# Head pairs in turns, three-pass scores and another tile order in the first output projection of a diffusion backbone

## The chip, the cores and the metric

The kernel runs on one core of a Trainium2 chip. The metric is the device time of one execution in microseconds, as the median of three runs. On the core, TensorE multiplies (its weight loads are shown as an engine of their own, PEld), VectorE (DVE), ScalarE (ACT) and GpSimd (POOL) compute, and SyncE (SP) and ScalarE issue the DMA transfers here. TensorE's results land in eight banks of PSUM, from which the other engines read.

## The reference

Two layers over 256 latent tokens of width 1024 and 256 context tokens. Each layer is a mixer and an expert retrieval (PEER), each behind a modulated RMS norm:

```python
f, p, q, k, v, gates = split_proj(h @ w_in[l])            # and the same for the context tokens
ya = latent_attention(q, k_all, v_all) @ attn_proj[l]     # 8 heads of 64, 2 key/value heads, keys of latents and context
yf, yp = fourier_branch(f, fourier_w[l]), pool_branch(p, ...)
x = x + m_lat[2] * merge(yf, yp, ya, gates, w_out[l])     # (gates[0]*yf + gates[1]*yp + gates[2]*ya) @ w_out
...
yac = attend(qc, kc, vc)                                  # context tokens see context keys; not in the last layer
x = x + m_lat[5] * peer(h2, peer_wq[l], peer_keys[l], peer_u[l], peer_v[l])

def attend(q, k, v):
    s = einsum('bqhgd,bkhd->bhgqk', q, k) * (HEAD_DIM ** -0.5)
    return einsum('bhgqk,bkhd->bqhgd', softmax(s), v)
```

Everything is float32. The last layer needs no context output, so it has two token tiles of 128 where layer 0 has four (tiles 0 and 1 latent, 2 and 3 context).

## The kernel before

**Arithmetic.** The large products are made of two halves: a matrix is split into a high part, rounded to `fp32r`, and the rest (`split_to`, L286 to L289: ScalarE copies the high part, VectorE or GpSimd subtracts). `mm3` (L281 to L284) then adds three single-speed matmuls, high by high, high by low and low by high. Products of plain float32 tiles run as two steps each on TensorE. In the attention, scores (L667) and value products (L700) are such float32 products.

**Weights.** `Stream` loads the weights in a fixed order through three `raw` tiles of 1 MB. `take` issues the loads of the tile taken and of the two behind it; `split` hands out a tile's two halves, and `presplit` splits the next item ahead of its use. SyncE issues these loads in the order in which the program names them, and a load waits until its `raw` tile was read.

**Attention.** `mixer` transposes keys into `kT` and queries into `qT` (64 rows for each head, two heads on 128 partitions) and goes over `items`: head pair `hc`, token tile `b`, head `e` of the pair. Layer 0 has 32 items, 16 of them wide (latent tiles, four key tiles) and 16 narrow (context tiles, two key tiles); layer 1 has 16 wide ones. A written pipeline spreads an item over four turns of the loop: `stage_scores` (product, maximum on VectorE, exponential with sum on ScalarE), `stage_norm` (scaling on VectorE), `stage_T` (transposes on TensorE, copy on ScalarE) and `stage_pv` (value products). Head `e` writes columns `64*e` to `64*e+63` of the array into the bank `ya`. Between these stages `fill` puts 32 steps of six gate matmuls each: eight ahead of the key transposes, 24 spread over the loop. Their results wait in the four gate buffers of `store`.

**Output projection, layer 0.** `wout(n, b)` makes columns `256*n` to `256*n+255` of token tile `b` (24 matmuls, then a product and a sum on VectorE, L1254 and L1255). `wout_end(b)` stores the tile (L1258) and computes its norm (`Norm.row`: square on ScalarE, L434, a chain of small operations on VectorE, L297 to L305, and the scaling L442). `Norm.trans` transposes a norm's tiles (L451); `Norm.cols` modulates them (L472, L474) and splits them into `hTh` and `hTl`, for the latents (0) or the context (1). `keys` transposes the retrieval keys (L1229). Behind this, `peer` begins: three conditioning products of the next layer (`ada_item`, L333), which use the first bank of a new PSUM layout, then the query products of the first retrieval head, over the latents' columns first (`h == 0`), then the context's `cols` and their columns.

**Order.** The order of the work on each engine is the order in which the program names it; there is no scheduler.

Of the kernel before, what the change touches and what calls it, by code (L numbers as in the profile page):

```python
# [60 lines left out]
def kernel(ctx_: ExitStack, tc: tile.TileContext, I, C, out):  # L61
    nc = tc.nc
# [32 lines left out]
    def b8(shape, dt=F32, name="b8"):  # L95
        return b8_p.tile(shape, dt, tag="b8", name=name)

    def b4(shape, dt=F32, name="b4"):
        return b4_p.tile(shape, dt, tag="b4", name=name)
# [4 lines left out]
    def psum(shape=(128, 512), dt=F32, name="ps"):  # L104
        return banks["ps"].tile(list(shape), dt, tag="ps", name=name)
# [374 lines left out]
    def mixer(l, nrm, last):  # L480
# [78 lines left out]
                nc.vector.tensor_tensor(out=v, in0=v, in1=rope[:, b, 0:1, :].to_broadcast([128, nh, HD]), op=OP.mult)  # L559
                nc.vector.tensor_tensor(out=src, in0=src, in1=t, op=OP.add)  # L560

        kT = b4([128, 512], name="kT")
        qT = b8([128, 4, nt], name="qT")
        for b in range(4):
            rot(b, KV[:, b, :128], 8, 2)
            if b < nq:
# [73 lines left out]
                yield from gate_sums(u, lambda c, ps, n=n: nc.scalar.activation(store[:, n, c, :], ps, AF.Copy), True)  # L640

        filler = fill()
        for _ in range(8):
            next(filler)
        ps = psum()
        for b in range(4):
            nc.tensor.transpose(ps[:, b * 128:(b + 1) * 128], KV[:, b, :128], ident)
        nc.scalar.activation(kT, ps, AF.Copy)
        for j in range(4):
            ps = psum()  # L650
            for b in range(nq):
                nc.tensor.transpose(ps[:, b * 128:(b + 1) * 128], P[:, b, 512 + j * 128:640 + j * 128], ident)
            nc.scalar.activation(qT[:, j, :], ps[:, :nt], AF.Copy)

        items = [(hc, b, e) for hc in range(4) for b in range(nq) for e in range(2)]
        st = {}
# [2 lines left out]
        def stage_scores(n):  # L659
            hc, b, e = items[n]  # L660
            h = 2 * hc + e
            v, j = divmod(h, 4)
            kb = (0, 4) if b < 2 else (2, 4)
            nk = (kb[1] - kb[0]) * 128
            ps = psum()
            s = slice(64 * v, 64 * v + 64)
            nc.tensor.matmul(ps[:, :nk], lhsT=qT[s, j, b * 128:(b + 1) * 128], rhs=kT[s, kb[0] * 128:kb[1] * 128],  # L667
                             start=True, stop=True)
            mx = small([128, 3], name="mx", bufs=6)
            nc.vector.tensor_reduce(out=mx[:, 0:1], in_=ps[:, :nk], op=OP.max, axis=AX)  # L670
            nc.vector.tensor_scalar(mx[:, 0:1], mx[:, 0:1], -0.125, None, op0=OP.mult)
            pm = ring[:, n % 4, :]
            nc.scalar.activation(pm[:, :nk], ps[:, :nk], AF.Exp, bias=mx[:, 0:1], scale=0.125, accum_out=mx[:, 1:2])
            st[n] = (pm, mx, kb, nk)
# [15 lines left out]
        ya = {}  # L690

        def stage_pv(n):
            hc, b, e = items[n]
            v = (2 * hc + e) // 4
            pT, kb = st.pop(n)
            if b == 0 and e == 0:
                ya[hc] = psum(name="ya")
            for q in range(kb[0], kb[1]):
                o = (q - kb[0]) * 128
                nc.tensor.matmul(ya[hc][64 * e:64 * e + 64, b * 128:(b + 1) * 128],  # L700
                                 lhsT=KV[:, q, 128 + 64 * v:192 + 64 * v], rhs=pT[:, o:o + 128],
                                 start=q == kb[0], stop=q == kb[1] - 1)
            if b == nq - 1 and e == 1:
                split_to(yh[:, 4 + hc, :], yl[:, 4 + hc, :], ya.pop(hc)[:, :nt])

        N = len(items)
# [1 line left out]
        if l:  # L708
            ffn_rows(l)
        for n in range(N + 3):  # L710
            if 0 <= n - 1 < N:
                stage_norm(n - 1)
            if n < N:
                stage_scores(n)
            while filled < min(24 * (n + 1) // N, 24):
                next(filler, None)
                filled += 1
            if 0 <= n - 2 < N:
                stage_T(n - 2)
            if n >= 3:  # L720
                stage_pv(n - 3)
        for _ in filler:
            pass
# [494 lines left out]
    for l in range(DEPTH):  # L1218
# [38 lines left out]
        def wout_end(b):  # L1257
            nc.sync.dma_start(out=xm[b], in_=X[:, b, :])  # L1258
            nrm.row(b // 2, b % 2)
# [5 lines left out]
                wout(n, b)  # L1265
        if nb == 4:
            wo[2] = S.split(("wout", l, 2))
            for b in range(nb):
                wout(2, b)
            wo[3] = S.split(("wout", l, 3))  # L1270
            kr = S.take(("keys", l)).rearrange("p (a d) -> p a d", d=128)
            for b in range(2):
                wout(3, b)
            wout_end(0)
            wout(3, 2)
            wout_end(1)
            S.presplit(True)
            wout(3, 3)
            kT = keys()
            for q in range(4):  # L1280
                nrm.trans(0, q)
            for b in (2, 3):
                wout_end(b)
            for q in range(4):
                nrm.cols(0, q)
        else:
            wo[2] = S.split(("wout", l, 2))
            wo[3] = S.split(("wout", l, 3))
            kr = S.take(("keys", l)).rearrange("p (a d) -> p a d", d=128)
            wout(2, 0)  # L1290
            wout(3, 0)
            wout_end(0)
            S.presplit(True)
            wout(2, 1)
            wout(3, 1)
            wout_end(1)
            kT = keys()
            for q in range(4):
                nrm.cols(0, q)
# [70 lines left out]
```

## Time and profile before

| | |
|---|---|
| median of 3 runs | 2943.49 us (2942.41 to 2950.72) |
| profiled execution | 2943.76 us; its span from first to last instruction 2942.0 us |
| busy share of the span | TensorE 94%, its loads 82%, VectorE 73%, ScalarE 47%, GpSimd 44% |
| mean granted TensorE clock | 0.97 of full speed |
| chain that ended last, by engine | TensorE 23%, VectorE 8%, DMA 5%, ScalarE 2% |

The page gives busy time by engine and the chain of work that ended last; the trace gives, for any stretch, the instructions in order of time, the idle time ahead of each and what ended it. Matmuls are pipelined: a row's length holds the way through the array, so what a matmul costs in a row of matmuls is read from start to start. The two attention loops are about 103 and 61 us of the span.

### The profile page before, as it was taken

What the parts mean: (1) busy time and instruction counts of PE and PEld (TensorE: products, weight loads), DVE (VectorE), ACT (ScalarE), POOL (GpSimd) and SP (SyncE); (2) the same over time, 40 slices, a digit from 0 to 9 for tenths busy, and PEclk for the clock granted to TensorE, in tenths of its full rate; (3) what the DMA queues carried; (4) which work ended last, traced back from release to release, by engine and by line L of the source; (5) the groups of instructions that cost most, each with busy time, mean ns of one, the idle gap of its engine ahead of it and who ended that gap; (6) DMA issues with size and microseconds to landing.
All of it is one profiled execution on the core that took longest, in us unless ns stands there. A gap on an engine that the chain in (4) does not pass through costs nothing. (4 is left out here: it accounts for less than half of the span.)

```text
span 2942.0 us, 42776 instructions
## 1 busy us (share of the span) xinstructions
PE 2753.4 (94%) x16484; PEld 2403.8 (82%) x16484; DVE 2158.2 (73%) x3388; ACT 1375.9 (47%) x2243; POOL 1282.2 (44%) x698
## 2 busy tenths in 40 slices
PE   6999998799899999999999997998989989899999
PEld 4767786689888889988888886788989989888887
DVE  3444344899999985589999996555988778566666
ACT  3343223134489983333333334545446766544443
POOL 0110003237777778676666662102677655500000
PEclk8999998899999999999999999999999999899999
DMA  6215756558999999999999994337788898967775
GB/s 232 87 44 177 253 186 187 157 120 210 258 286 296 291 297 286 268 361 377 379 376 380 369 362 173 119 123 189 157 194 191 223 223 208 249 250 299 280 296 198
DMA packets 365580, 706.99 MB, mean 240 GB/s; under 512 B 25424, under 2 KB 265456, under 8 KB 351296
## 3 DMA queue, kind: packets, MB, share of 16 engines
q1 hardware_dynamic: 271104, 491.38, 56.0%
q0 software_dynamic: 36864, 134.23, 12.5%
q10 hardware_dynamic: 57408, 78.65, 7.9%
q8 instruction: 129, 2.11, 0.3%
q14 instruction: 75, 0.61, 0.1%
HBM read 619.18 MB, written 85.00 MB: 239 GB/s over the span
## 5 line engine op out<-in xcount | busy, mean ns | idle before, releaser
L1180 PE MATMUL acc<-hl,A 128*128 128x512 f32 x3840 | 871.2, 389 | 0.0
L1180 PEld LDWEIGHTS acc<-hl,A 128*128 128x128 f32 x3840 | 720.6, 188 | 150.1 <-ACT A L287 0.5
L1025 POOL TENSOR_TENSOR hl<-UT,hl 128x1024 fp32r<-128x1024 f32 x256 | 629.1, 2483 | 301.0 <-ACT hl L1018 298.9
L289 POOL TENSOR_TENSOR hl<-raw,hl 128x1024 fp32r<-128x1024 f32 x112 | 277.9, 2492 | 695.4 <-ACT hl L287 575.6
L287 ACT ACTIVATE hl<-raw 128x1024 fp32r<-128x1024 f32 x388 | 387.9, 1048 | 251.2 <-PE acc L1180 77.6
L289 DVE TENSOR_TENSOR hl<-raw,hl 128x1024 fp32r<-128x1024 f32 x276 | 349.8, 1299 | 133.5 <-ACT hl L287 133.2
L1011 DVE STREAM_TRANSPOSE UT<-raw 128x2048 f32<-128x2048 f32 x128 | 294.3, 2301 | 173.1 <-DMA raw<-in_peer_u_dram 115.0
L282 PE MATMUL ps<-hTh,hl 128*128 128x384 f32 (+2 forms) x1168 | 407.9, 349 | 4.2 <-ACT hl L1018 4.2
L284 PE MATMUL ps<-hTh,hl 128*128 128x384 f32 (+2 forms) x1168 | 402.0, 344 | 6.1 <-POOL hl L1025 6.1
L283 PE MATMUL ps<-hTl,hl 128*128 128x384 f32 (+2 forms) x1168 | 401.7, 344 | 3.5 <-POOL hTl L289 3.5
L284 PE MATMUL ps<-hT,hl 128*128 128x256 f32 x1152 | 333.7, 290 | 9.8 <-POOL hl L1025 9.8
L282 PE MATMUL ps<-hT,hl 128*128 128x256 f32 x1152 | 337.7, 293 | 1.6 <-ACT hl L1018 1.6
L283 PE MATMUL ps<-hT,hl 128*128 128x256 f32 x1152 | 333.3, 289 | 1.1 <-POOL hT L289 1.1
L1018 ACT ACTIVATE hl<-UT 128x1024 fp32r<-128x1024 f32 x256 | 256.6, 1051 | 140.1 <-DVE UT L1011 116.8
L287 ACT ACTIVATE A<-af 128x768 fp32r<-128x768 f32 (+1 forms) x128 | 94.4, 738 | 333.3 <-PE acc L1180 178.2
L282 PEld LDWEIGHTS ps<-hTh,hl 128*128 128x128 f32 x1168 | 224.8, 192 | 20.9 <-issue 4.9
L284 PEld LDWEIGHTS ps<-hT,hl 128*128 128x128 f32 x1152 | 228.4, 198 | 11.6 <-POOL hl L1025 11.6
L284 PEld LDWEIGHTS ps<-hTh,hl 128*128 128x128 f32 x1168 | 224.6, 192 | 12.1 <-POOL hl L1025 7.4
L283 PEld LDWEIGHTS ps<-hTl,hl 128*128 128x128 f32 x1168 | 225.1, 193 | 8.0 <-POOL hTl L289 3.7
L282 PEld LDWEIGHTS ps<-hT,hl 128*128 128x128 f32 x1152 | 229.6, 199 | 2.0 <-ACT hl L1018 2.0
L289 DVE TENSOR_TENSOR A<-af,A 128x768 fp32r<-128x768 f32 (+1 forms) x128 | 142.9, 1117 | 119.5 <-ACT A L287 119.5
L283 PEld LDWEIGHTS ps<-hT,hl 128*128 128x128 f32 x1152 | 229.0, 199 | 1.6 <-POOL hT L289 1.6
(245 smaller groups left out, 4795.8 us busy)
## 6 DMA issues: line engine op xcount, KB each, us to landing
raw<-in_peer_u_dram SPq DMA_DIRECT2D x512, 256.0 KB
raw<-in_peer_v_dram SPq DMA_DIRECT2D x128, 1024.0 KB
raw<-in_ada_w_dram SPq DMA_DIRECT2D x48, 1024.0 KB
G<-stg ACTq DMA_DIRECT2D x20, 2048.0 KB
raw<-in_w_in_dram SPq DMA_DIRECT2D x34, 1024.0 KB
Gq<-G SPq DMA_DIRECT2D x16, 1536.0 KB
H<-Hg ACTq DMA_DIRECT2D x56, 384.0 KB
Hq<-H SPq DMA_DIRECT2D x14, 1536.0 KB
```

The source lines that it names most:

```text
L282: nc.tensor.matmul(ps, lhsT=lh, rhs=rh, start=first, stop=False)
L283: nc.tensor.matmul(ps, lhsT=lh, rhs=rl, start=False, stop=False)
L284: nc.tensor.matmul(ps, lhsT=ll, rhs=rh, start=False, stop=last)
L287: nc.scalar.activation(hi, src, AF.Copy)
L289: eng.tensor_tensor(out=lo, in0=src, in1=hi.bitcast(F32), op=OP.subtract)
L1011: nc.vector.transpose(t, r)
L1018: nc.scalar.activation(t[:, 0, a], v[:, a], AF.Copy)
L1025: nc.gpsimd.tensor_tensor(out=t[:, 1, a], in0=v[:, a], in1=t[:, 0, a].bitcast(F32), op=OP.subtract)
L1180: nc.tensor.matmul(acc[b][n], lhsT=a4[:, lhs, a, t], rhs=rhs[:, o:o + 512], start=f, stop=e)
```

## The change

Four edits, all in the program's order or in the form of its products:

- `kT` and `qT` become pairs of high and low halves (`split_to` out of PSUM, with VectorE's subtraction), and a score is three `mm3` matmuls in place of one float32 product.
- `stage_pv` runs every second turn and does both heads of a pair, key tile by key tile, head 0 and head 1 in turns.
- In the loop `stage_scores(n)` stands ahead of `stage_norm(n - 1)`; of the eight filler steps ahead of the transposes four stay there, and one stands behind each of the four groups of query transposes.
- In layer 0's output projection the last two column blocks go tile by tile for the latents, then the context tiles; the keys' transposes, the latents' transposes and `cols` are placed between the context's products.

The gate buffers (`fills`, `store`) are the same before and after.

```diff
-        for _ in range(8):
+        for _ in range(4):
             next(filler)
         ps = psum()
         for b in range(4):
             nc.tensor.transpose(ps[:, b * 128:(b + 1) * 128], KV[:, b, :128], ident)
-        nc.scalar.activation(kT, ps, AF.Copy)
+        kT = [b4([128, 512], F32R, name="kT") for _ in range(2)]
+        qT = [b8([128, 4, nt], F32R, name="qT") for _ in range(2)]
+        split_to(kT[0], kT[1], ps)
         for j in range(4):
             ps = psum()
             for b in range(nq):
                 nc.tensor.transpose(ps[:, b * 128:(b + 1) * 128], P[:, b, 512 + j * 128:640 + j * 128], ident)
-            nc.scalar.activation(qT[:, j, :], ps[:, :nt], AF.Copy)
+            split_to(qT[0][:, j, :], qT[1][:, j, :], ps[:, :nt])
+            next(filler)
...
-            nc.tensor.matmul(ps[:, :nk], lhsT=qT[s, j, b * 128:(b + 1) * 128], rhs=kT[s, kb[0] * 128:kb[1] * 128],
-                             start=True, stop=True)
+            qh, ql = (t[s, j, b * 128:(b + 1) * 128] for t in qT)
+            kh, kl = (t[s, kb[0] * 128:kb[1] * 128] for t in kT)
+            mm3(ps[:, :nk], qh, ql, kh, kl, True, True)
...
         def stage_pv(n):
-            hc, b, e = items[n]
-            v = (2 * hc + e) // 4
-            pT, kb = st.pop(n)
-            if b == 0 and e == 0:
+
+            hc, b, _ = items[n]
+            v = 2 * hc // 4
+            if b == 0:
                 ya[hc] = psum(name="ya")
+            two = [st.pop(n - 1), st.pop(n)]
+            kb = two[0][1]
             for q in range(kb[0], kb[1]):
                 o = (q - kb[0]) * 128
-                nc.tensor.matmul(ya[hc][64 * e:64 * e + 64, b * 128:(b + 1) * 128],
-                                 lhsT=KV[:, q, 128 + 64 * v:192 + 64 * v], rhs=pT[:, o:o + 128],
-                                 start=q == kb[0], stop=q == kb[1] - 1)
-            if b == nq - 1 and e == 1:
+                for e, (pT, _) in enumerate(two):
+                    nc.tensor.matmul(ya[hc][64 * e:64 * e + 64, b * 128:(b + 1) * 128],
+                                     lhsT=KV[:, q, 128 + 64 * v:192 + 64 * v], rhs=pT[:, o:o + 128],
+                                     start=q == kb[0], stop=q == kb[1] - 1)
+            if b == nq - 1:
...
         for n in range(N + 3):
+            if n < N:
+                stage_scores(n)
             if 0 <= n - 1 < N:
                 stage_norm(n - 1)
-            if n < N:
-                stage_scores(n)
...
-            if n >= 3:
+            if n >= 3 and n % 2 == 0:
                 stage_pv(n - 3)
...
             wo[2] = S.split(("wout", l, 2))
-            for b in range(nb):
-                wout(2, b)
             wo[3] = S.split(("wout", l, 3))
             kr = S.take(("keys", l)).rearrange("p (a d) -> p a d", d=128)
             for b in range(2):
+                wout(2, b)
                 wout(3, b)
-            wout_end(0)
+                wout_end(b)
+            S.presplit(True)
+            wout(2, 2)
             wout(3, 2)
-            wout_end(1)
-            S.presplit(True)
-            wout(3, 3)
             kT = keys()
+            wout(2, 3)
             for q in range(4):
                 nrm.trans(0, q)
+            for q in range(4):
+                nrm.cols(0, q)
+            wout(3, 3)
             for b in (2, 3):
                 wout_end(b)
-            for q in range(4):
-                nrm.cols(0, q)
```

TensorE in layer 0's attention, before, where the loop passes from wide to narrow items (`ring` holds the exponentials and their transposes, `gate` is the filler; a row's x counts matmuls of the program; a value product and a score of before are two steps each on TensorE):

```order
L685 MATMUL ps<-ident,ring 128x128 x4
L700 MATMUL ya<-ring,KV 64x128 x4
L667 MATMUL ps<-kT,qT 128x256
L685 MATMUL ps<-ident,ring 128x128 x4
L700 MATMUL ya<-ring,KV 64x128 x4
L667 MATMUL ps<-kT,qT 128x256
L282 MATMUL gate<-hTh,hl 128x512
```

The same place in the changed kernel:

```order
L282 MATMUL ps<-kT,qT 128x256
L283 MATMUL ps<-kT,qT 128x256
L284 MATMUL ps<-kT,qT 128x256
L687 MATMUL ps<-ident,ring 128x128 x4
L705 MATMUL ya<-ring,KV 64x128 x8
L282 MATMUL ps<-kT,qT 128x256
L283 MATMUL ps<-kT,qT 128x256
L284 MATMUL ps<-kT,qT 128x256
L282 MATMUL gate<-hTh,hl 128x512
```

Two groups of four value products, each behind its own transposes, became one of eight, and a score became three matmuls.

VectorE at the end of layer 0's output projection, before (`tm` and `X` are the last product's two operations, `na` to `xn` tile 3's norm, `hTf` and `hTl` the latents' columns):

```order
L1254 TENSOR_TENSOR tm<-ps,mrow 128x256
L1255 TENSOR_TENSOR X<-X,tm 128x256
L297 TENSOR_SCALAR na<-ss 128x1
L300 RECIPROCAL nr<-nr 128x1
L302 TENSOR_TENSOR nt<-nr 128x1
L303 TENSOR_TENSOR nt<-nt,na 128x1
L304 TENSOR_SCALAR nt<-nt 128x1
L305 TENSOR_TENSOR nr<-nr,nt 128x1
L442 TENSOR_SCALAR xn<-X,nr 128x4x8x32
```

The same engine in the changed kernel, from the latents' columns on:

```order
L472 TENSOR_SCALAR hTf<-ps,sc_2907,col_2905 128x256 x2
L289 TENSOR_TENSOR hTl<-hTf,hTh 128x2x256
L472 TENSOR_SCALAR hTf<-ps,sc_2907,col_2905 128x256 x2
L289 TENSOR_TENSOR hTl<-hTf,hTh 128x2x256
L1259 TENSOR_TENSOR tm<-ps,mrow 128x256
L1260 TENSOR_TENSOR X<-X,tm 128x256
L297 TENSOR_SCALAR na<-ss 128x1
L300 RECIPROCAL nr<-nr 128x1
```

The latents' columns, which stood behind the norms of tiles 2 and 3, now stand ahead of the last product's two operations and of both norms.

## Rows read from the trace of the kernel before

**Rows 1.** Windows: both attention loops, the idle stretch, the conditioning products; busy us.

```profile
core 0: us, PE busy (x) PEld busy (x) DVE busy (x) ACT busy (x) POOL busy (x), PEclk, DMA share, GB/s
135.20:238.60 103.40, 102.40 (x497) 66.45 (x496) 44.50 (x131) 47.52 (x114) 15.26 (x8) 1.00 0.11 37
1873.40:1934.00 60.60, 60.48 (x368) 42.79 (x368) 27.85 (x67) 31.17 (x67) 16.09 (x7) 1.00 0.22 70
446.60:455.30 8.70, 0.03 (x3) 0.04 (x3) 6.29 (x19) 5.49 (x14) 2.88 (x3) 0.70 0.94 347
455.30:460.50 5.20, 5.20 (x24) 1.09 (x24) 1.14 (x1) 0.40 (x1) 1.48 (x2) 0.51 0.23 70
```

**Rows 2.** Timeline of TensorE, layer 0's loop: start us, length us, line, shape, count.

```profile
151.70 1.09 PE L700 MATMUL ya<-ring,KV 128*64 128x128 f32 x8
152.72 0.70 PE L667 MATMUL ps<-kT,qT 64*128 64x256 f32 x2
153.34 0.50 PE L282 MATMUL gate<-hTh,hl 128*128 128x512 f32 x1
153.68 0.39 PE L283 MATMUL gate<-hTl,hl 128*128 128x512 f32 x1
153.91 0.39 PE L284 MATMUL gate<-hTh,hl 128*128 128x512 f32 x1
...
158.59 0.65 PE L700 MATMUL ya<-ring,KV 128*64 128x128 f32 x4
159.17 1.12 PE L667 MATMUL ps<-kT,qT 64*128 64x512 f32 x2
```

**Rows 3.** Timeline of TensorE, layer 1's loop, its first score.

```profile
1873.44 1.12 PE L667 MATMUL ps<-kT,qT 64*128 64x512 f32 x2
1874.49 0.38 PE L282 MATMUL gate<-hTh,hl 128*128 128x256 f32 x1
1874.71 0.28 PE L283 MATMUL gate<-hTl,hl 128*128 128x256 f32 x1
1874.83 0.28 PE L284 MATMUL gate<-hTh,hl 128*128 128x256 f32 x1
```

**Rows 4.** Timeline of TensorE: Fourier products (full columns) and band products (two halves).

```profile
112.20 3.62 PE L592 MATMUL ps<-p,raw 128*128 128x256 f32 x16
115.75 3.73 PE L604 MATMUL ps<-raw,P 128*64 128x256 f32 x32
```

**Rows 5.** Timeline of TensorE behind layer 0's output projection; in brackets idle time before.

```profile
442.97 1.91 PE L1229 MATMUL ps<-ident,raw 128*128 128x128 f32 x16
...
455.29 5.29 PE L333 MATMUL adaps<-raw,cT 128*32 128x512 f32 x24 [8.67 <-DVE hTf L472]
460.50 0.39 PE L282 MATMUL ps<-hTh,hl 128*128 128x256 f32 x1
```

**Rows 6.** Timelines of ScalarE and VectorE: the latents' columns, first and later operations.

```profile
449.98 1.00 ACT L474 ACTIVATE hTf<-ps,col,sc 128x256 f32<-128x256 f32 x2
...
453.43 0.69 DVE L289 TENSOR_TENSOR hTl<-hTf,hTh 128x512 fp32r<-128x512 f32 x1 [0.70 <-ACT hTh L287]
...
455.73 1.14 DVE L289 TENSOR_TENSOR hTl<-hTf,hTh 128x512 fp32r<-128x512 f32 x1 [0.70 <-ACT hTh L287]
```

**Rows 7.** Timeline of SyncE's DMA issues: third conditioning tile, next query weights.

```profile
447.99 0.33 SPq L198 DMA_DIRECT2D raw<-in_ada_w_dram  x1
...
458.37 1.80 SPq L204 DMA_DIRECT2D raw<-in_peer_wq_dram  x4
```

**Rows 8.** Timelines of ScalarE, GpSimd and TensorE: what the context's columns wait for.

```profile
465.71 2.01 ACT L287 ACTIVATE hl<-raw 128x1024 fp32r<-128x1024 f32 x2 [10.01 <-DMA raw<-in_peer_wq_dram]
...
466.85 4.67 POOL L289 TENSOR_TENSOR hl<-raw,hl 128x1024 fp32r<-128x1024 f32 x2 [10.07 <-ACT hl L287]
...
473.24 0.58 PE L283 MATMUL ps<-hTl,hl 128*128 128x256 f32 x1 [3.52 <-POOL hTl L289]
```

**Rows 9.** Instructions on tile `mx`: the scaling of L679, ns min/median/max.

```profile
L679 DVE TENSOR_SCALAR ring<-ring,mx x48: 352/486/2186, 139.6 to 1929.2; 128x512 f32<-128x512 f32 x32, 128x256 f32<-128x256 f32 x16
```

More of the change, by code (lines that the diff above doesn't have):

```diff
@@ L560, in rot @@
                 nc.vector.tensor_tensor(out=src, in0=src, in1=t, op=OP.add)
-        kT = b4([128, 512], name="kT")
-        qT = b8([128, 4, nt], name="qT")
         for b in range(4):
```

## The prediction

> **What bounds the kernel now.** I read the stretches first, then the matmuls in order of time in each stretch that the change touches, then the queues around the one hole found there. [rows 1] give the two attention loops (layer 0 from the first score at 135.2 us to 238.6, layer 1 from 1873.4 to 1934.0): TensorE is busy 102.4 of 103.4 us and 60.5 of 60.6 at the full clock, while VectorE, ScalarE and GpSimd are each busy less than 53% of the time and the DMA engines 11 and 22%. So what these loops cost is what TensorE issues in them, and what is taken off TensorE there comes off the loop as long as VectorE and ScalarE keep up. Nothing is prefetched further meanwhile, since three raw tiles are all there are, so a shorter loop shifts what follows and takes nothing from it. The end of layer 0's output projection is another kind of place: [rows 5] show TensorE done with the projection at 442.97, then transposing, then idle for the 8.67 us ahead of 455.29 (so from 446.6) until VectorE has read the last transposed norm tile, then three conditioning products in 5.2 us, and the first query product at 460.50. In that hole and behind it the granted clock is 0.70 and 0.51 [rows 1]: the lower level (1.2 GHz, against 2.4) stands from inside the hole until the query products start.
>
> **Value products in turns.** Start to start, a wide item (four key tiles, eight steps on TensorE since each float32 product is two) takes 151.70 to 152.72 = 1.02 us, a narrow one (two key tiles) 158.59 to 159.17 = 0.58 [rows 2]. The difference of four steps is 0.44, so a step is 0.11 and 0.14 is fixed (entry and exit). Now all steps of one head go to one half of the columns, and the other half idles. The change puts the two heads of a pair, which write the two halves, behind each other product by product. What two halves in turns are worth stands in [rows 4]: 16 steps of 256 columns with full 128-column weights take 3.62 us (0.23 each), and 32 steps of the same length with 64-column weights that go to both halves take 3.73 (0.12 each). So two halves run side by side there, their weight loads too, and I take it that a pair costs what one item costs now. Layer 0 has 8 wide and 8 narrow pairs: 8 x 1.02 + 8 x 0.58 = 12.8 us. Layer 1 has 8 wide pairs: 8.2. Together **21.0 us**.
>
> This speaks against a rule. The Trainium skill, page "TensorE: Matmul & The Clock Gate", section "Part 3: Packing small matmuls — row/col tiling", says that a weight load is pulled ahead of running matmuls only where the row group differs, and here both heads use all rows. By that rule each step would show its load; the trace of the band products does not agree (0.12 us a step with both halves in use). It is rival A below.
>
> **Scores in three passes.** A wide score takes 1873.44 to 1874.49 = 1.05 us [rows 3], a narrow one 152.72 to 153.34 = 0.62 [rows 2]. Both are two steps, so 256 columns more cost 0.215 a step, a wide step 0.43, a narrow one 0.215, and 0.19 is fixed (the load after the change from 128 to 64 rows, and the way out). Three single-speed passes follow each other at 0.23 us for 512 columns (153.68 to 153.91) and 0.12 for 256 (1874.71 to 1874.83). New: 3 x 0.23 + 0.19 = 0.88, and 3 x 0.12 + 0.19 = 0.55. Layer 0 saves 16 x 0.17 + 16 x 0.07 = 3.8, layer 1 16 x 0.17 = 2.7: **6.6 us**. No row shows these passes on 64 rows; if each showed its load, at most the fixed 0.19 again for two of them, it would be 48 x 0.38 = 18 us less, which I think unlikely since the second load of today's score is hidden in its first step.
>
> **What it adds.** Five more VectorE subtractions per layer for the low halves of keys and queries, about 0.7 us each (the subtraction of 453.43 in [rows 6]), stand ahead of the loop; four of the eight filler steps that stood ahead of the transposes now stand between them and behind the last. Each filler step is six gate matmuls at 0.23, some 1.4 us, so the first score's inputs have 5 us of cover: nothing. Without it they would cost 2 to 3 us. In the loop the maximum of item n now stands ahead of the norm of item n-1 on VectorE; that takes a wait for the exponential out of VectorE's way and costs TensorE nothing. At the end of each loop the last pair waits for its last copy with no other head's products ahead of it: 0 to 1 us, I take 0.5 in each layer, **+1.0**. Nine or so short waits of TensorE for copies in today's loops may go (up to 2 us); I count none.
>
> **Latent tiles first.** The products and transposes of the output projection are the same, so TensorE reaches the end of the last one (now tile 3's last columns, behind the transposes) at the same place, about 446.5. What changes is what is late then. The latent transposes end three products earlier, and the chain that turns them into column form, 449.98 to 456.9 now [rows 6], can start at 442.5; it should take a us less, since VectorE is not in tile 3's norm at its start, and end at about 448.4, beside tile 3's product. The conditioning product needs VectorE to have read that product's bank, which VectorE does behind the chain: 448.8, against 455.29. That is 6.5 us, and at the full clock the three take 2.6 instead of 5.2. Against it stands SyncE's queue. The third of those tiles is loaded behind the store of tile 3, which waits for the last product; it now issues at 447.99 [rows 7] and would issue at 449.4. How long such a load takes no row bounds closely: the query load issued from 458.37 is used at 465.71, 7.3 us; I take 4.6, so 454.0. The next query load's last quarter waits for the same landing and then lands at about 457, against 465.71 [rows 8]. From there on it is today's chain: ScalarE splits it, GpSimd is busy for 4.67 us with the low half, and only then does the context tiles' first low half release TensorE, at 473.24 now. That gives 8.7 us; since TensorE waits twice (2.3 and 3.5 us) ahead of the query products and may fall to the lower clock for part of 5.8 us of work, I take **7.5 us**, with 3 and 11 as the ends. What is late next is the same GpSimd split.
>
> **The sum.** 21.0 + 6.6 - 1.0 + 7.5 = 34.1 us. The profiled execution took 2943.8 us (span 2942.0), 0.3 over the median of 2943.5: 2943.5 - 34.1 = 2909.4, I say **2909.5**.
>
> **Rivals.**
> A, loads show: if half of the fixed 0.14 is a load and every step shows it, a step is 0.18, a wide pair 8 x 0.18 + 0.07 = 1.51 against 2.04, a narrow one 0.79 against 1.16; 16 x 0.53 + 8 x 0.37 = 11.4 instead of 21.0: 2919. Against it: [rows 4].
> B, the projection's order brings nothing: SyncE's store of tile 3 holds the loads back for as long as the hole is now, or the lower clock eats it: 2917. For it: ScalarE already waits 10.01 us for that load in [rows 8].
> C, VectorE and ScalarE become the bound in the loops: a scaling that takes 0.49 us in the middle takes up to 2.19 [rows 9], and GpSimd, which I suspect behind it, works 15 us and 16 us in these loops. With a seventh of layer 0's 32 items and a quarter of layer 1's 16 hit, 9 x 1.7 = 15 us come back: 2925. Against it: VectorE is at 43 and 46% [rows 1], and its maximum no longer waits behind the norm.
> D, slower than before: a change between column halves costs what the entry into the value products costs now, 0.14, instead of nothing. The place is each product of a pair: a wide pair is then 8 x 0.14 + 16 x 0.11 = 2.88 us against 2.04, a narrow one 1.44 against 1.16, 15.7 us more instead of 21.0 less: 2946. It is slower than before from about 0.12 us a change, and over 0.3% slower from 0.18. Against it: the band products change halves at 0.12 us a step, all included.
>
> **How the numbers follow.** The forecast, with its terms inside their ends, 0.73 (2901 to 2916); A 0.05, B 0.12, C 0.06, D 0.02, and 0.02 for what I don't see, as no change. The range 2901 to 2919 holds the forecast, A and B. A measurement of this kernel can tell about 0.3%, or 9 us, from no change. All but D and the unseen are faster by more: faster 0.95; of the rest 0.04 same, 0.01 slower.
>
> **What would show it.** In the profile of the changed kernel: the 16 steps of a wide pair of value products should stand in about 1.0 us, in twos; 2.0 would be wrong, 1.5 rival A. A wide score should be followed 0.88 us later by the next matmul. The loops should last about 87 and 50 us with TensorE still over 97% busy; if it isn't, C. Behind the output projection the idle time ahead of the first conditioning product should be 2 to 3 us instead of 8.67, a new wait for the third conditioning tile should show, and the wait for GpSimd's low half should come 7 to 8 us sooner, measured from the end of the last projection product. Equal loop times would make the prediction wrong by its larger part, a later query stage by its smaller.

## The result, and the profile of the changed kernel

The changed kernel takes **2907.83 us** (median of five runs, 2906.67 to 2910.68) beside 2943.49 for the kernel before on the same chip: a ratio of 0.9879, with a 95% interval of 0.9865 to 0.9893, or 35.7 us less where 34.1 were forecast. Its profiled execution has a span of 2908.7 us, 33.3 less than before.

The stretches of the two attention loops, from the first score to the last value product (columns as in [rows 1]):

```profile
135.10:222.70 87.60, 86.90 (x533) 61.98 (x533) 44.24 (x132) 46.50 (x112) 15.49 (x8) 1.00 0.13 44
1852.80:1904.10 51.30, 50.91 (x385) 39.73 (x384) 29.67 (x70) 30.02 (x65) 16.67 (x7) 1.00 0.26 83
```

Against [rows 1] the loops are 15.9 and 9.3 us shorter (103.4 to 87.5, 60.6 to 51.3; the forecast was "about 87 and 50"), and TensorE is busy 99% of both. The timeline of TensorE in layer 0's loop shows a wide score, a wide pair of value products, a narrow pair, and the last pair of the loop; the last three rows are the last pair of layer 1's loop:

```profile
138.31 0.49 PE L282 MATMUL ps<-kT,qT 64*128 64x512 f32 x1
...
139.20 0.50 PE L282 MATMUL gate<-hTh,hl 128*128 128x512 f32 x1
...
145.27 1.09 PE L705 MATMUL ya<-ring,KV 128*64 128x128 f32 x16
146.29 0.38 PE L282 MATMUL ps<-kT,qT 64*128 64x256 f32 x1
...
155.84 0.66 PE L705 MATMUL ya<-ring,KV 128*64 128x128 f32 x8
156.43 0.50 PE L282 MATMUL ps<-kT,qT 64*128 64x512 f32 x1
...
221.49 0.43 PE L705 MATMUL ya<-ring,KV 128*64 128x128 f32 x2
222.09 0.65 PE L705 MATMUL ya<-ring,KV 128*64 128x128 f32 x6 [0.17 <-ACT ring L689]
222.67 1.92 PE L333 MATMUL adaps<-raw,cT 128*32 128x512 f32 x16
...
1902.27 0.43 PE L705 MATMUL ya<-ring,KV 128*64 128x128 f32 x2
1903.09 1.09 PE L705 MATMUL ya<-ring,KV 128*64 128x128 f32 x14 [0.39 <-ACT ring L689]
1904.11 0.39 PE L282 MATMUL ps<-y,hl 128*128 128x256 f32 x1
```

Read from start to start, 16 steps of a wide pair take 1.02 us, where [rows 2] have 8 steps of one item in 1.02; 8 steps of a narrow pair take 0.59, where one item's 4 took 0.58. In the single records behind the row at 145.27 the steps start in twos, 0.007 us apart, and the twos follow each other at 0.109. A wide score is followed after 0.89 us.

The last pairs wait for ScalarE's copy of the second head. From their first step to the product behind them they take 1.18 us (221.49 to 222.67, a narrow pair) and 1.84 us (1902.27 to 1904.11, a wide one), so 0.6 and 0.8 us more than an undisturbed pair. The bracketed idle times, 0.17 and 0.39, show less than that, since they count from the modelled end of the matmul before. The pair before the last loses 0.38 in each layer, and one wide pair in layer 0's loop (166.69) loses 0.96.

Behind layer 0's output projection, whose last product ends at 430.69, TensorE does this:

```profile
432.89 2.99 PE L333 MATMUL adaps<-raw,cT 128*32 128x512 f32 x16 [2.20 <-ACT junk L434]
439.77 1.93 PE L333 MATMUL adaps<-raw,cT 128*32 128x512 f32 x8 [3.89 <-DMA raw<-in_ada_w_dram]
441.63 0.58 PE L282 MATMUL ps<-hTh,hl 128*128 128x256 f32 x1
...
452.32 0.38 PE L283 MATMUL ps<-hTl,hl 128*128 128x256 f32 x1 [1.10 <-POOL hTl L289]
```

The wait of 8.67 us in [rows 5] is 2.20 now, and a new one of 3.89 stands ahead of the third conditioning tile. The stretches (columns as in [rows 1]) of the first two conditioning tiles and of the third show a granted clock of 0.62 and 0.50, so the three still take 4.9 us (2.99 and 1.86) where [rows 1] have 5.2:

```profile
432.90:436.00 3.10, 2.98 (x16) 0.58 (x16) 2.35 (x11) 1.45 (x4) 0.00 (x0) 0.62 0.67 211
439.80:441.70 1.90, 1.90 (x9) 0.24 (x9) 0.00 (x0) 0.00 (x0) 0.00 (x0) 0.50 1.12 203
```

SyncE's queue (start, length, issues) and the two engines behind it show why the new wait is there:

```profile
425.53 8.07 SPq L1263 DMA_DIRECT2D xm<-X  x2
433.65 0.43 SPq L198 DMA_DIRECT2D raw<-in_ada_w_dram  x1
...
436.18 3.88 SPq L204 DMA_DIRECT2D raw<-in_peer_wq_dram  x4
```

```profile
445.16 2.01 ACT L287 ACTIVATE hl<-raw 128x1024 fp32r<-128x1024 f32 x2 [9.56 <-DMA raw<-in_peer_wq_dram]
```

```profile
446.30 4.74 POOL L289 TENSOR_TENSOR hl<-raw,hl 128x1024 fp32r<-128x1024 f32 x2 [14.16 <-ACT hl L287]
```

The stores of tiles 2 and 3 hold SyncE for 8.07 us; the third tile's load is issued at 433.65 and used at 439.77. Against the end of all that TensorE has of the projection and its transposes (446.62 before, 430.69 now) the first conditioning product comes 6.5 us sooner (8.67 to 2.20 behind it), the query weights' split 4.6 (19.1 to 14.5, [rows 8]) and the wait for GpSimd's low half 5.0 (26.6 to 21.6, [rows 8]). What came 6.5 us sooner is partly given back two steps later.

Cut at TensorE's own work, the 33.3 us of the two profiles are: layer 0's loop 15.9, from its end to the first one-hot product of layer 0's retrieval 6.7, layer 1's loop 9.3, and 1.4 in all the rest. In that rest one stretch moves by itself: from the first to the last one-hot product (`ps<-ohs`) of layer 1's retrieval, where VectorE waits some 40 us for rows of `peer_u`, 287.5 us before and 284.0 after. In the profiles of the experiments, whose code there is the same, it is between 274.5 and 286.4. So a whole time says little about a few microseconds; below, the length of a loop or a wait decides, and the whole time stands beside it.

### The profile page after: what moved, and what is told of

Same layout as the page of the kernel before. It is cut to its first block, busy times and chain, and to the rows that moved or that the text cites. A ratio compares the mean times of both kernels' runs of the same rounds, so it can differ in the third digit from the quotient of the medians.

```text
span 2908.7 us, 42894 instructions
## 1 busy us (share of the span) xinstructions
PE 2723.7 (94%) x16532; PEld 2391.5 (82%) x16532; DVE 2160.5 (74%) x3398; ACT 1375.2 (47%) x2243; POOL 1279.2 (44%) x698
```

## The experiments

Each kernel ran in several rounds beside the kernel before on the same chip. Loops are from the first score to the first product behind the last value product, in the profiled execution. Medians of two lines can come from two chips (the kernel before has 2941.71 to 2944.41 there), so lines are compared by their ratios, and differences of medians below are rough.

| kernel | loop, layer 0 | loop, layer 1 | median us | ratio to before [95%] |
|---|---|---|---|---|
| before | 103.4 | 60.6 | 2943.49 | |
| changed | 87.5 | 51.3 | 2907.83 | 0.9879 [0.9865, 0.9893] |
| e1 value products in turns alone | 94.0 | 54.5 | 2925.48 | 0.9941 [0.9923, 0.9960] |
| e2 scores alone | 100.5 | 58.6 | 2929.50 | 0.9951 [0.9935, 0.9966] |
| e3 projection alone | 103.4 | 60.6 | 2939.47 | 0.9981 [0.9969, 0.9993] |
| e4 pairs without turns | 90.9 | 54.1 | 2915.22 | 0.9908 [0.9891, 0.9924] |
| e5 norm ahead of scores | 94.2 | 53.1 | 2913.97 | 0.9903 [0.9885, 0.9921] |
| e6 load ahead | 87.5 | 51.3 | 2903.07 | 0.9868 [0.9848, 0.9887] |
| e7 no cover | 88.0 | 51.6 | 2909.82 | 0.9878 [0.9861, 0.9895] |
| e8 row halves | 81.4 | 46.7 | 2893.32 | 0.9823 [0.9806, 0.9840] |
| e9 row halves and load ahead | 82.2 | 48.0 | 2897.23 | 0.9838 [0.9824, 0.9851] |
| e10 other buffers | 103.4 | 60.6 | 2942.32 | 1.0003 [0.9991, 1.0016] |
| e11 splits on VectorE | 102.3 | 58.7 | 2929.31 | 0.9951 [0.9935, 0.9966] |
| e12 e9 with splits on VectorE | 82.6 | 48.8 | 2898.25 | 0.9861 [0.9839, 0.9884] |

### One edit at a time

**Value products alone.** The kernel before, with `stage_pv` of the change, called every second turn.

> The kernel before with the value products of a pair in turns alone. By the prediction: a wide pair of 16 steps in 1.02 us, a narrow one of 8 in 0.58, the loops 103.4 - 12.3 = 91.1 and 60.6 - 7.7 = 52.9 us, the whole 20 us less than before (2923.5). Rival A (each step shows its load): 11.4 us less, 2932. Rival D (a change of half costs 0.14): 15.7 us more, 2959.

The pairs cost 1.02 and 0.59 us, as forecast, but the loops save 9.4 and 6.1 us instead of 12.3 and 7.7. TensorE's timeline in layer 0's loop shows the difference:

```profile
145.49 0.63 PE L685 MATMUL ps<-ident,ring 128*128 128x128 f32 x4 [0.46 <-DVE ring L679]
...
147.49 1.09 PE L703 MATMUL ya<-ring,KV 128*64 128x128 f32 x14 [1.00 <-ACT ring L687]
```

Where no filler stands between the turns, TensorE is now ahead of the scaling and of the copy: 2.5 us of waits in this loop, against 0.7 in the changed kernel's. Rivals A and D are out; something else of the change is needed to get the rest of the gain.

**Scores alone.** The kernel before, with the halves of `kT` and `qT`, `mm3` in `stage_scores`, and four filler steps moved behind the transposes.

> The kernel before with scores in three passes alone (halves of keys and queries, four filler steps behind the transposes). By the prediction: a wide score followed after 0.88 us instead of 1.05, a narrow one after 0.55 instead of 0.62, loops 3.8 and 2.7 us shorter, the whole 6.6 us less (2936.9). If VectorE's five more subtractions or the split's waits show: 2 to 5 us less only.

A wide score is followed after 0.89 us, a narrow one after 0.55, and the loops save 3.0 and 2.0 us, of 3.8 and 2.7 forecast; 1.8 us of waits for ScalarE's copies are in layer 0's. The whole saves 14.6 us, though, and in the profile 13.0 us of its 20 stand in layer 1's retrieval (274.5 us against 287.5), which no line of this edit touches. All six executions (2923.78 to 2935.25) lie under the lowest of before (2938.61), so it isn't one odd execution.

**Other buffers.** One thing that the scores' edit does to later code is to take two more buffers, after which later tiles fall on other ones.

```diff
         qT = b8([128, 4, nt], name="qT")
+        b4([128, 512], name="kT")
+        b8([128, 4, nt], name="qT")
```

> The kernel before with one more buffer each of the kinds that kT and qT use taken and left unused, so that later tiles fall on the buffers on which they fall with scores in three passes; every instruction is that of before. The scores alone measured 14.6 us less, of which their loops show 5.0. If the other buffers bring the rest: 5 to 10 us less than before (2934 to 2938). If the rest is the unsteady length of layer 1's retrieval (274 to 288 us in the profiles so far): as before, 2943.

Nothing: 1.0003, with 286.4 us in that retrieval. The buffers aren't it, and why the scores' edit shortened the retrieval stays open.

**Projection alone.**

> The kernel before with the new tile order of layer 0's output projection alone. By the prediction: 7.5 us less (2936.0), with the wait for GpSimd's low half 7 to 8 us sooner behind the projection. From the trace of the changed kernel: that wait comes 5.0 us sooner behind the projection's end and the saving is about 5 us (2938.5). Rival B: nothing (2943.5).

4.7 us less by the medians (interval 2 to 9). In its profile the same waits stand as in the changed kernel (2.19 and 4.37 ahead of the conditioning products), GpSimd's low half is waited for 5.9 us sooner than before in absolute time, 0.9 of which had come ahead of the loop, and the first one-hot product comes 6.7 us sooner behind the loop. Rival B (nothing) is out; 7.5 was a little too much.

### What in the value products pays

**Pairs without turns.**

```diff
-            for q in range(kb[0], kb[1]):
-                o = (q - kb[0]) * 128
-                for e, (pT, _) in enumerate(two):
+            for e, (pT, _) in enumerate(two):
+                for q in range(kb[0], kb[1]):
+                    o = (q - kb[0]) * 128
```

> The changed kernel, but inside a pair all key tiles of head 0 go first, then all of head 1: the same products, paired, without turns. If turns between the column halves are what pays: 24 pairs go back to two heads behind each other, less one entry of 0.14 each: wide pairs 1.9 us, narrow ones 1.0, some 17 to 18 us more than the changed kernel (2925). If the pairing alone (fewer changes of product kind) is what paid: as the changed kernel, 2908.

Neither. TensorE's timeline, a wide pair and a narrow one:

```profile
144.49 1.58 PE L705 MATMUL ya<-ring,KV 128*64 128x128 f32 x16
146.00 0.38 PE L282 MATMUL ps<-kT,qT 64*128 64x256 f32 x1
...
162.24 0.66 PE L705 MATMUL ya<-ring,KV 128*64 128x128 f32 x8
162.83 0.50 PE L282 MATMUL ps<-kT,qT 64*128 64x512 f32 x1
```

A wide pair takes 1.51 us, between 1.02 (in turns) and 2.04 (two items); a narrow pair takes 0.59 without any turns. The single records say how: head 1's first step, which its weight load's wait for a semaphore marks, starts at 144.985, while three of head 0's eight steps are still to start (145.088, 145.197, 145.306, by their spacing of 0.109). So TensorE itself looks a few products ahead and starts what goes to the idle half of the columns. Pairing alone brings all of the gain where a head has four steps and half of it where it has eight; writing them in turns brings the other half, 0.49 us for a wide pair. For eight such pairs in each layer that is 3.9 us twice; the loops are 3.4 and 2.8 us longer than the changed kernel's, the whole 7.4. What is missing falls on the pairs that wait for ScalarE's copy in either kernel: the wide one of layer 0 that loses 0.96, and the last of layer 1.

### The order in the loop

**Norm ahead of the scores.** The one edit that the prediction valued at nothing, undone.

```diff
+            if 0 <= n - 1 < N:
+                stage_norm(n - 1)
             if n < N:
                 stage_scores(n)
-            if 0 <= n - 1 < N:
-                stage_norm(n - 1)
```

> The changed kernel with the norm of item n-1 again ahead of the scores of item n in the loop. By the prediction that order costs TensorE nothing: loops 87.5 and 51.3 us, 2908. Against it stand the runs of the single edits: their loops save 9.4 + 3.0 and 6.1 + 2.0 us, 3.5 and 1.2 less than the changed kernel's 15.9 and 9.3, and TensorE waits 2.5 us in the loop of the value products alone against 0.7. If the order is what the difference is: loops 91 and 52.5 us, 2912.5.

It costs more than either case says: loops 6.7 and 1.8 us longer, the whole 6.1. TensorE's timeline, VectorE's, and two stretches of layer 0's loop:

```profile
145.17 0.63 PE L687 MATMUL ps<-ident,ring 128*128 128x128 f32 x4 [1.04 <-DVE ring L681]
...
147.16 1.97 PE L705 MATMUL ya<-ring,KV 128*64 128x128 f32 x14 [1.00 <-ACT ring L689]
```

```profile
140.89 0.16 DVE L680 RECIPROCAL mx<-mx 128x1 f32<-128x1 f32 x1 [0.85 <-ACT ring L675]
141.09 0.49 DVE L681 TENSOR_SCALAR ring<-ring,mx 128x512 f32<-128x512 f32 x1
141.49 0.68 DVE L672 TENSOR_REDUCE mx<-ps 128x1 f32<-128x512 f32 x1
...
143.21 0.16 DVE L680 RECIPROCAL mx<-mx 128x1 f32<-128x1 f32 x1 [0.85 <-ACT ring L675]
143.41 1.62 DVE L681 TENSOR_SCALAR ring<-ring,mx 128x512 f32<-128x512 f32 x1
```

```profile
143.90:147.20 3.30, 1.25 (x10) 0.67 (x9) 2.38 (x5) 1.98 (x5) 3.30 (x2) 0.95 0.00 0
147.20:153.70 6.50, 6.50 (x27) 4.93 (x27) 2.41 (x9) 1.62 (x5) 0.03 (x1) 0.50 0.45 161
```

With the norm first, the maximum of an item (L672) waits on VectorE behind the scaling of the item before, which waits for that item's exponential, which had waited for its maximum: one item after the other, 2.32 us apart (140.89 to 143.21). That is short enough for the kernel before, where a wide turn without filler takes TensorE 2.60 us (score 1.05, transposes 0.53, value products 1.02); it is too long for the changed kernel's 1.93 (0.89, 0.53, and half a pair, 0.51). TensorE waits 2.04 us in 3.3, and then works for 6.5 us at a granted clock of 0.50 (the lower level, 1.2 GHz). The half speed costs some 3.3 us, more than the waits. So the changed order guards 8.5 us of the loops' gain. No run has it alone in the kernel before; it could pay little there, where TensorE is busy 102.40 of 103.40 us [rows 1].

**The splits on VectorE.** The scaling of 143.41 took 1.62 us instead of 0.49, beside GpSimd's subtractions. This kernel keeps the order just shown and moves those to VectorE.

```diff
-            return r, self.presplit_steps(True)
+            return r, self.presplit_steps()
```

> The norm ahead of the scores in the loop as in e5_norm_first, but the low halves of the gate weights that are split inside the loops are subtracted on VectorE, so that GpSimd does nothing there. If GpSimd's subtractions are what stretches VectorE's scalings (0.49 us in the middle, up to 1.6): no scaling of 512 columns over 0.6 us, no wait for one, and the loops back at about 88 and 51.5 us from 94.2 and 53.1 (2908). If the order itself is the wait: loops as in e5_norm_first, 2914.

The first half held, the second didn't. The 48 scalings (ns, min/median/max):

```profile
L681 DVE TENSOR_SCALAR ring<-ring,mx x48: 352/486/492, 139.3 to 1928.3; 128x512 f32<-128x512 f32 x32, 128x256 f32<-128x256 f32 x16
```

With GpSimd idle none takes over 0.492 us. In the fourteen profiles together 102 of 672 scalings take over 0.52 us, and each of these overlaps an instruction of GpSimd and ends 0.14 to 0.29 us behind the end of one: GpSimd's work is what stretches them. The changed kernel has 11 of them, of 0.63 to 1.71 us, and none of TensorE's waits in its loops is for VectorE. But here the loops became 102.3 and 58.7 us. VectorE and TensorE around the worst wait:

```profile
147.24 1.23 DVE L289 TENSOR_TENSOR hl<-raw,hl 128x1024 fp32r<-128x1024 f32 x1 [1.79 <-ACT hl L287]
148.57 0.49 DVE L681 TENSOR_SCALAR ring<-ring,mx 128x512 f32<-128x512 f32 x1
```

```profile
149.21 1.09 PE L687 MATMUL ps<-ident,ring 128*128 128x128 f32 x4 [3.21 <-DVE ring L681]
```

VectorE's queue now stands 1.79 us for ScalarE's high half and works 1.23 on the low one, with the scaling that TensorE needs behind it. TensorE waits 7.2 us in layer 0's loop, and the granted clock is 0.54 from 151.2 to 158.0. The cure was worse than the stretched scaling. Since it puts a new wait into VectorE's queue, it doesn't tell how the 8.5 us of the norm ahead divide between the order and the stretched scalings; that stays open.

**Without cover.**

```diff
-        for _ in range(4):
+        for _ in range(8):
             next(filler)
...
             split_to(qT[0][:, j, :], qT[1][:, j, :], ps[:, :nt])
-            next(filler)
```

> The changed kernel with all eight filler steps ahead of the transposes and none behind them, so that nothing covers the splits of keys and queries. By the prediction TensorE then waits 2 to 3 us ahead of the first score in each layer: 2912 to 2914. If the splits were not late in any case: as the changed kernel, 2908.

2909.82 us, as the changed kernel. TensorE goes from the last transposes straight into the first score:

```profile
132.88 1.91 PE L652 MATMUL ps<-ident,P 128*128 128x128 f32 x16
134.72 0.49 PE L282 MATMUL ps<-kT,qT 64*128 64x512 f32 x1
```

The first score needs only the first of the four groups of query transposes, and the other three are cover enough for its split. The price of 2 to 3 us for lost cover was wrong; the split costs at most the 0.5 and 0.3 us by which these loops are longer.

### Behind the projection

**The load ahead.**

```diff
+            S.ahead(S.n + 3)
             wout(3, 3)
             for b in (2, 3):
                 wout_end(b)
```

> The changed kernel with the load of the third conditioning tile issued ahead of the last product and of the stores of tiles 2 and 3. If SyncE's queue is what made the term of the projection too large: TensorE's 3.89 us wait for that tile is gone, the first query product comes 3.9 us sooner behind the projection (7.0 instead of 10.9 us), the wait for GpSimd's low half 2 to 4 us sooner (2905). If the transfers themselves are late (the DMA engines are 93% busy there) or the raw tile is still being read: a wait of the same size in the same place, 2908.

SyncE now issues the load at 425, ahead of the stores, and TensorE's timeline is:

```profile
432.72 4.48 PE L333 MATMUL adaps<-raw,cT 128*32 128x512 f32 x24 [2.18 <-ACT junk L434]
437.12 0.39 PE L282 MATMUL ps<-hTh,hl 128*128 128x256 f32 x1
...
450.60 0.58 PE L283 MATMUL ps<-hTl,hl 128*128 128x256 f32 x1 [3.51 <-POOL hTl L289]
```

The 3.89 us are gone and the first query product is 4.4 us nearer to the projection's end (6.6 against 10.9). The wait for GpSimd's low half grows from 1.10 to 3.51, and by the retrieval's first one-hot product 0.3 us is left. So the queue was the cause of that wait, and the next wait takes its gain: ScalarE, and GpSimd behind it, start when the next query weights have landed (ScalarE at 443.08 instead of 445.16, for issues from 435.36 instead of 436.18). The whole reads 4.8 us less by the medians and 3.2 by the ratios, with an interval that overlaps the changed kernel's; in this profile layer 1's retrieval took 278.1 us, 5.9 less.

### A version that beats both

**Row halves.** If two halves of the columns run side by side, two halves of the rows may. A score uses the 64 rows of its key head; pairing heads of different key heads gives the two scores of a pair different rows, and heads of different parity still write different columns.

```diff
-        items = [(hc, b, e) for hc in range(4) for b in range(nq) for e in range(2)]
+        items = [(h, b) for two in ((0, 5), (1, 4), (2, 7), (3, 6)) for b in range(nq) for h in two]
...
+            for i in range(3):
+                for ps, p in got:
+                    nc.tensor.matmul(ps[:, :nk], lhsT=p[i][0], rhs=p[i][1], start=i == 0, stop=i == 2)
```

> The changed kernel with heads paired across the two key heads (0 and 5, 1 and 4, 2 and 7, 3 and 6) and the three passes of both scores in turns: the two heads of a pair then use the two halves of the rows, and still write the two halves of the columns in the value products. If row halves run side by side as column halves do: two wide scores in about 0.9 us instead of 1.76, two narrow ones in 0.57 instead of 1.08, loops 11 and 7 us shorter, 2890. If only one entry of 0.19 in two is saved: 4.6 us, 2903. If halves of the rows don't run together and a change of half shows its load: 4 more loads of 0.1 in each pair, 10 us more than the changed kernel.

2893.32 us, 0.9823 [0.9806, 0.9840]: faster than the changed kernel, with intervals that don't touch. TensorE's timeline, and the stretches of the loops:

```profile
135.71 0.96 PE L673 MATMUL ps<-kT,qT 64*128 64x512 f32 x6
136.60 0.50 PE L282 MATMUL gate<-hTh,hl 128*128 128x512 f32 x1
...
144.71 0.63 PE L694 MATMUL ps<-ident,ring 128*128 128x128 f32 x4 [2.08 <-DVE mx L687]
```

```profile
135.70:217.10 81.40, 76.81 (x530) 55.35 (x529) 43.15 (x131) 45.80 (x112) 15.33 (x8) 0.98 0.14 47
1849.60:1896.30 46.70, 43.75 (x386) 35.68 (x385) 28.88 (x68) 29.94 (x64) 16.35 (x7) 1.00 0.28 92
```

The six passes of two wide scores take 0.89 us, as long as one score's three. The loops gain 6.1 and 4.6 us of the 11 and 7 that this is worth; the rest is waits (TensorE 94% busy, against 99%) and, in layer 0, a stretch at a lower granted clock behind them (0.85):

```profile
148.20:154.50 6.30, 6.30 (x41) 4.86 (x40) 2.47 (x10) 2.57 (x8) 0.00 (x0) 0.85 0.37 146
```

Ahead of it two scalings of 2.4 us stand beside GpSimd's subtractions (VectorE, then GpSimd; last, all scalings of this kernel in ns):

```profile
142.14 2.42 DVE L688 TENSOR_SCALAR ring<-ring,mx 128x512 f32<-128x512 f32 x1
...
144.66 2.40 DVE L688 TENSOR_SCALAR ring<-ring,mx 128x512 f32<-128x512 f32 x1
```

```profile
141.92 4.86 POOL L289 TENSOR_TENSOR hl<-raw,hl 128x1024 fp32r<-128x1024 f32 x2 [8.92 <-ACT hl L287]
```

```profile
L688 DVE TENSOR_SCALAR ring<-ring,mx x48: 352/486/2711, 140.0 to 1890.7; 128x512 f32<-128x512 f32 x32, 128x256 f32<-128x256 f32 x16
```

Here rival C has come true, one step beyond the change. The two scalings end at 144.56 and 147.06, both 0.28 us behind one of GpSimd's two subtractions (144.28 in the single records, and 146.78). By the Trainium skill, page "SBUF — State Buffer", section "SBUF: two separate sides", VectorE and GpSimd share a pair of ports as an exclusive lock: a VectorE operation that uses the pair, as a `tensor_scalar` like this scaling can, or a GpSimd one holds it for its whole instruction while the other waits. The trace agrees in these two rows and in the 102 stretched scalings counted above, and the kernel with GpSimd idle shows none stretched.

**With the load ahead, and with the splits moved.**

> The changed kernel with row halves in turns (e8_row_halves) and the third conditioning load ahead (e6_load_ahead), GpSimd keeping the splits in the loops. The loops as in e8_row_halves, 81.4 and 46.7 us. Behind the projection as in e6_load_ahead: no wait for the third conditioning tile, first query product 6.6 us behind the last projection product. If what e6_load_ahead gained by its time (4.8 us) was the load: 2888.5. If it is given back behind GpSimd's low half, as its trace shows (0.3 us left at the first retrieval), and the rest was the unsteady retrieval of layer 1: 2893.

> The changed kernel with row halves in turns (e8_row_halves), the third conditioning load ahead (e6_load_ahead) and the loops' splits on VectorE instead of GpSimd. If GpSimd's subtractions are what stretches the scalings: the 4.6 and 3 us of waits for VectorE and the gate halves in the loops of e8_row_halves go, loops 77 and 44 us from 81.4 and 46.7, and the whole is 7 us under e8_row_halves, 2886. If VectorE's 1.3 us for each of 16 halves fills it instead: loops as long as in e8_row_halves or longer, 2893 or more.

Neither adds to it: 2897.23 and 2898.25 us. The interval of the first overlaps that of the row halves alone; that of the second touches it at its edge only, with loops 3.3 us longer, so moving the splits is the worse of the two. The load ahead again brings the first query product nearer, to 6.3 and 6.6 us behind the projection, and the whole times show nothing of it. With both, the loops are 0.8 and 1.3 us longer than with the row halves alone, though their code is the same: TensorE waits no longer in them (4.2 and 2.9 us, against 4.6 and 3.0), but 6.8 and 3.4 us of them ran at a granted clock of 0.50, against 3.4 and none. So what equal waits cost by the clock differs from profile to profile. The splits on VectorE again trade stretched scalings for a queue that stands (4.2 us of waits for the scaling in layer 0's loop).

## Why the prediction was right, step by step

- **A pair costs what one item cost.** Right: 1.02 and 0.59 us, in twos. Reading the price off the band products ([rows 4]) held. It left out that TensorE would find part of the overlap without turns.
- **Scores.** Right: 0.89 and 0.55 us for 0.88 and 0.55; three passes on 64 rows show no loads.
- **The loops' sums.** 16.1 forecast for layer 0 (12.8 + 3.8 - 0.5) and 15.9 measured; 10.4 for layer 1 (8.2 + 2.7 - 0.5) and 9.3 measured. The term for the ends of the loops was too small: 0.5 us each, where the last two pairs lose 1.0 us in layer 0 and 1.2 in layer 1, by their starts. In layer 0 another pair loses 0.96, and the sum still came out because the transposes of before, with their short waits, took 1.4 us more (15.2 against 13.8 in the loop), which the prediction counted as none. In layer 0 that is luck.
- **"That costs TensorE nothing", of the order in the loop.** The step that failed, without harm to the sum. It was valued by what it removes from a loop in which VectorE keeps up, not from the loop that the other edits leave. Undone, it takes back 8.5 us of the loops' 25.2. Rival C named the mechanism, VectorE late with stretched scalings, at 2925 for the whole; without this edit the whole was 2914, and how much of that is the stretched scalings isn't shown.
- **Cover of the splits.** Nothing, as forecast; the price without it was wrong (under 1 us instead of 2 to 3).
- **Latent tiles first.** 7.5 forecast with ends 3 and 11; 5.0 at GpSimd's low half and 6.7 at the retrieval. The idle time ahead of the first conditioning product (2.2 us for "2 to 3") and the new wait behind SyncE's store came as written. Two terms were mis-sized: the third tile's load took 6.1 us from issue to use where 4.6 was taken, and the query weights were split 4.6 us sooner where 8.7 was taken. The three conditioning products, 2.6 us "at the full clock", took 4.9 at granted clocks of 0.62 and 0.50, so the lower clock that the prediction allowed for came. That rival B's queue holds the loads back is true for 3.89 us, and the load ahead shows that this alone is worth nearly nothing.
- **The rest.** 35.7 us by the medians are 25.2 of the loops, 6.7 of the projection and about 4 that no step of the prediction holds; in the two profiles 3.5 us stand in layer 1's retrieval, whose length moves by more than that between kernels with the same code there, and 2.1 go the other way elsewhere. Of the forecast 34.1 us its own steps brought 31.9, so that forecast and result lie only 1.7 us apart is partly luck.

## What to carry to other kernels

Two matmuls that use different halves of the array, of its columns or of its rows, cost here what one costs; write them next to each other, and look for operands that can be regrouped so that neighbours fall on different halves. When TensorE's part of a pipelined loop is shortened, work out anew what one item's chain through the other engines takes (here 2.32 us), since a queue order that was free before can then set the pace. And a wait put ahead of TensorE can cost more than its length, since the clock may fall behind it; one taken away can be given back at the next load.

## What the runs showed of the hardware

- TensorE started products for the idle half of the columns out of the program's order: with eight steps of each head written one head after the other, head 1's first started with three of head 0's still to come; with four and four the whole overlap was found (0.59 us).
- Six passes of 512 columns on two row halves in turns took 0.89 us, as three on one half.
- Two waits of 1.04 and 1.00 us within 3.3 us were followed by 6.5 us at a granted clock of 0.50; the changed kernel, with 0.7 us of waits in the whole loop, kept 1.00 throughout.
- A scaling of 512 columns on VectorE takes 0.49 us, up to 2.71 with row halves in turns, where it stands beside GpSimd subtractions, and never over 0.492 with GpSimd idle. Of 672 scalings of 512 or 256 columns in all profiles, the 102 over 0.52 us all end 0.14 to 0.29 us behind the end of a GpSimd instruction.
